# Half of a weight pair's combinations formed by an accumulating DMA, and another order of the seven products

## The chip, the cores and the metric

The kernel runs on one core of a Trainium2 chip. The metric is the device time of one execution in microseconds, as the median of several runs. TensorE (PE), VectorE (DVE), ScalarE (ACT), GpSimd (POOL) and the DMA queue of SyncE (SP) each work through their own list of instructions in order, and wait for each other by semaphores.

## What is computed

The reference runs two blocks on a sequence of 512 tokens of width 1024. The first has two layers modulated by a condition vector (one with differential attention and a gated delta rule, one with neighbourhood attention); the second has 2 hybrid layers (forgetting attention beside retention). All four layers end in a gated feed-forward network (FFN), and it is there, and in the projections that feed the hybrid layers, that the changed code works:

```python
def hybrid_layer(h, attn_norm_g, w_in, b_fgate, ret_gn_g, w_out,
                 ffn_norm_g, w_gate, w_up, w_down, cos, sin):
    xn = rmsnorm(h, attn_norm_g)
    proj = jnp.einsum('bld,dc->blc', xn, w_in)
    ...
    hn = rmsnorm(h, ffn_norm_g)
    ff = jax.nn.silu(jnp.einsum('bld,df->blf', hn, w_gate)) * jnp.einsum('bld,df->blf', hn, w_up)
    return h + jnp.einsum('blf,fd->bld', ff, w_down)
```

## The kernel before

Every large product is taken in full precision out of three passes: a weight tile and an activation are each split into a high part (ScalarE casts, into `whi`) and a low part (VectorE subtracts, into `wlo` for weights), and TensorE multiplies high by high, high by low and low by high.

**A pair by seven products.** For the gate and the up projection of an FFN, one 128-column tile of `w_gate` and one of `w_up` form a pair, `ra` and `rb`, each 128 x 1024 (eight blocks of the contraction over 128). The tokens are cut in two halves, the contraction in two halves (columns 0 to 511 and 512 to 1023 of a tile: a0, a1 of `ra`, b0, b1 of `rb`). Instead of eight half-size products the function `seven` does seven, out of sums of weight quarters and sums of activation quarters (the latter made once per layer by `make_quads` and `end_quads`, lines to L861). One such product is 4 x 3 = 12 matmuls with 128x256 outputs (L890), a pair 84. The weight sums are formed on GpSimd, in f32: L872 writes the high half of `s23` (a0 - b0), L873 adds b1 onto b0 in place (the sum is called rb' here), L874 writes the low half of `s23` (rb' - a0), L875 writes `s4` (a1 minus that low half). Then come, in program order, the split of `ra` and the products p1, p2; the split of `s23` and p6, p7; the split of `rb` and p5, p4; the split of `s4` and p3. ScalarE casts at L880, VectorE makes the low part at L881. Between the products the results are added: `u` is a copy of p1 (L901), L905 adds p6 to it, L909 makes v of p5 and u, L910 adds p7 to u, and `put` (L931) adds a last product and stores one quarter of the result; SiLU is at L933, gate times up at L936, the split of the hidden tile at L938 and L939.

**Where pairs stand.** Each of the four FFNs has 22 pairs of tiles. The first three go by another, slower way while the quarter sums of the activations are made; the other 19 go through `fast_pair`, which loads the two tiles (L924, L925) and calls `seven`. They stand in groups (one pair left of the first four; then 4, 4, 4 and 6). After every pair `work` runs down projections of the group before (`fm_group`, load L446, cast L462, low part L463, matmul L592, 24 matmuls each): two per pair in groups of four, one per pair for the last four pairs of the last group. `hy_two` does 10 pairs in each of the two hybrid layers, with its own loads (L1657).

**Buffers.** Raw weight tiles rotate through four buffers `wraw`, high and low parts through three each (`top.whi_65` to `67`, `top.wlo_68` to `70`). `s23` and `s4` take rings `ws` (1024 wide) and `w4` (512 wide), two buffers each in an FFN and one each in the hybrid layers. At the start of an FFN these rings lie in memory that the making of the activations' quarter sums still holds; L861 (`end_quads`) and L727 (the slow way's hidden tile) are VectorE's last instructions on it.

**Order.** A scheduler reorders the instructions of each engine by priorities, with the program order as a base; what an engine does next is then fixed. In the middle of an FFN TensorE's order per pair is p1 p2 p6 p7 p5 p4 p3 and two down projections. `ra` lies in the third high buffer, `s23` in the first, `rb` in the second; `s4` takes the third when p1 has read its half.

Of the kernel before, what the change touches and what calls it, by code (L numbers as in the profile page):

```python
# [16 lines left out]
ALU = mybir.AluOpType  # L17
# [6 lines left out]
T = 512  # L24
# [202 lines left out]
class K:  # L227
# [635 lines left out]
            T[1][1].append(dl)  # L863
        self.free(first)

    def seven(self, ra, rb, hi, lo, quads, h, put):


        nc = self.nc
        T = quads[0]  # L870
        s23, s4 = self.ring("ws"), self.ring("w4")
        nc.gpsimd.tensor_sub(s23[:, 512:], ra[:, :512], rb[:, :512])  # L872
        nc.gpsimd.tensor_add(rb[:, :512], rb[:, :512], rb[:, 512:])  # L873
        nc.gpsimd.tensor_sub(s23[:, :512], rb[:, :512], ra[:, :512])  # L874
        nc.gpsimd.tensor_sub(s4, ra[:, 512:], s23[:, :512])  # L875

        def split(src):
            m = src.shape[-1]
            wh, wl = self.weight("whi"), self.weight("wlo")
            nc.scalar.copy(wh[:, :m], src)  # L880
            nc.vector.tensor_sub(wl[:, :m], src, wh[:, :m].bitcast(F32))  # L881
            return wh, wl

        def product(w, o, x):
            ps = self.ps("L")[:, :h]
            for k in range(4):
                wc = slice(o + k * P, o + (k + 1) * P)
                for ww, xx, st, sp in ((w[0], x[0], k == 0, False), (w[0], x[1], False, False),
                                       (w[1], x[0], False, k == 3)):
                    nc.tensor.matmul(ps, ww[:, wc], xx[k], start=st, stop=sp)  # L890
            return ps

        def part(k0, c0):
            return [[x[k][:, c0:c0 + h] for k in range(k0, k0 + 4)] for x in (hi, lo)]

        t = self.ring("sp")
        u, v = t[:, :h], t[:, h:2 * h]
        w = split(ra)
        p1 = product(w, 0, part(0, 0))
        p2 = product(w, 512, part(4, 0))  # L900
        nc.scalar.copy(u, p1)  # L901
        put(0, 0, p2, u)
        w = split(s23)
        p6 = product(w, 0, T[2])
        nc.vector.tensor_add(u, p6, u)  # L905
        p7 = product(w, 512, T[3])
        w = split(rb)
        p5 = product(w, 0, T[1])
        nc.vector.tensor_add(v, p5, u)  # L909
        nc.vector.tensor_add(u, p7, u)  # L910
        put(1, 1, p7, v)
        p4 = product(w, 512, T[4])
        put(1, 0, p4, u)
        w = split(s4)
        p3 = product(w, 0, part(4, h))
        put(0, 1, p3, v)

    def fast_pair(self, gate, up, hi, lo, quads, h, hh, hl):

        nc = self.nc  # L920
        self.stream("L", "ffn")
        n = 2 * h
        rg, ru = self.weight("wraw"), self.weight("wraw")
        nc.sync.dma_start(rg, gate)  # L924
        nc.sync.dma_start(ru, up)  # L925
        sg, su = self.ring("sg"), self.ring("su")

        def put(tile, half, ps, more):
            c = slice(half * h, half * h + h)
            dst = (su if tile else sg)[:, c]  # L930
            nc.vector.tensor_add(dst, ps, more)  # L931
            if not tile:
                nc.scalar.activation(dst, dst, AF.Silu)  # L933

        self.seven(rg, ru, hi, lo, quads, h, put)
        nc.vector.tensor_mul(sg[:, :n], sg[:, :n], su[:, :n])  # L936
        th, tl = self.rslot("hh"), self.rslot("hl")
        nc.scalar.copy(th[:, :n], sg[:, :n])  # L938
        nc.vector.tensor_sub(tl[:, :n], sg[:, :n], th[:, :n].bitcast(F32))  # L939
        hh.append(th)  # L940
        hl.append(tl)
# [702 lines left out]
    def hy_two(self, l, js, hi, lo, outs, acts=(AF.Copy, AF.Copy)):  # L1644

        nc = self.nc
        quads = self.hyq
        if quads is None:
            for j, o, act in zip(js, outs, acts):
                def evict(i, ps, c0):  # L1650
                    nc.scalar.activation(o[:, c0:c0 + ps.shape[1]], ps, act)
                self.hy_tile(l, j, hi, lo, evict)
            return
        h = TB // 2
        ra, rb = self.weight("wraw"), self.weight("wraw")
        for t, j in zip((ra, rb), js):
            nc.sync.dma_start(t, self.a["w_hy"][l, j])  # L1657

        def put(tile, half, ps, more):
            dst = outs[tile][:, half * h:half * h + h]  # L1660
            nc.vector.tensor_add(dst, ps, more)
            if acts[tile] != AF.Copy:
                nc.scalar.activation(dst, dst, acts[tile])

        self.seven(ra, rb, hi, lo, quads, h, put)

    def v_tokens(self, f, stream):

# [168 lines left out]
    def ret_head(self, l, h, q, k, v, gate):  # L1837
# [45 lines left out]
        for i in range(5):  # L1883
# [18 lines left out]
                 w4=(512, 2)), LIN[1])  # L1902
# [495 lines left out]
```

## Time and profile before

| | us |
|---|---|
| median of 3 runs | 3403.38 |
| runs, lowest and highest | 3396.11, 3406.44 |
| profiled execution | 3402.65 |
| its span in the trace | 3400.7 |
| TensorE busy in the span | 3261.2 |
| VectorE, ScalarE, GpSimd busy | 2373.1, 1478.8, 879.7 |

The span is what the trace covers; the profiled execution's own time is 1.95 us longer. Four stretches of the span are the FFNs from their first fast pair on: 720 to 1000, 1680 to 1970, 2380 to 2640 and 3060 to 3350 us. What lies between is attention, recurrences, norms and projections. Idle time of an engine other than TensorE is of interest only where TensorE waits for it. GpSimd's idle time in the table of waits is for the most part a wait for a pair's tiles to land.

### The profile page before, as it was taken

The page shows a single profiled execution, that of the slowest core. Times are in us where ns is not written, and L with a number is a line of the kernel's source. Part 1 is how long each engine was busy: PE and PEld are TensorE (multiplying, and loading weights), DVE is VectorE, ACT ScalarE, POOL GpSimd, SP SyncE. Part 2 cuts the span into 40 slices and gives each one's busy share as a digit, 9 for nine tenths or more (in the row PEclk, how much of TensorE's full clock was granted, in tenths as well). Part 3 has the DMA queues.
Part 4 walks back from the last instruction along what each step waited for, and adds up shares of the span by engine and source line. Part 5 has one row for each costly group of instructions (what it writes and reads, how often), then busy time and mean ns, then how long its engine had stood idle before and what let it go on. Part 6 is the DMA issues. An engine that isn't in the chain of part 4 may idle for free.

```text
span 3400.7 us, 64156 instructions
## 1 busy us (share of the span) xinstructions
PE 3261.2 (96%) x25466; PEld 3021.2 (89%) x25466; DVE 2373.1 (70%) x4863; ACT 1478.8 (43%) x2767; POOL 879.7 (26%) x772
## 2 busy tenths in 40 slices
PE   7999999989999999999899999999999999999998
PEld 6877777789999789998899998879999988799998
DVE  7566757677786565445777876877777667788775
ACT  4455442354444344434544444434444444344444
POOL 0000252023342011110233432423333224313332
PEclk9999989999999999999999999999999999999999
DMA  5111254523334874111233342223333412132332
GB/s 219 43 37 61 87 174 152 167 91 100 103 109 145 308 235 129 60 49 43 90 104 102 99 150 66 66 73 97 100 103 100 158 51 69 57 119 88 103 106 92
DMA packets 144348, 365.95 MB, mean 108 GB/s; under 512 B 30368, under 2 KB 33440, under 8 KB 144048
## 3 DMA queue, kind: packets, MB, share of 16 engines
q1 hardware_dynamic: 136704, 352.63, 32.1%
q10 hardware_dynamic: 7344, 9.23, 0.9%
q8 instruction: 200, 3.28, 0.4%
q14 instruction: 100, 0.82, 0.1%
HBM read 342.75 MB, written 19.04 MB: 106 GB/s over the span
## 4 chain that ended last, share of the span: by engine, by line
PE 73%; DVE 9%; issue 4%; ACT 3%; DMA 3%; POOL 1%; DVEq 0%; ACTq 0%; POOLq 0%; SPq 0%
PE ffn.L L592 22%; PE ffn.L L890 21%; PE outp.L L592 4%; PE naproj.L L656 3%; PE retproj.L L890 3%; PE gproj.L L592 3%; PE foxproj.L L890 2%; PE foxproj.L L592 2%; PE fox.A L1794 1%; DVE top.wlo L881 1%; PE ret.B L1871 1%; PE fox.Ao L1820 1%; PE naattn.Ao L1626 1%; PE retproj.L L592 1%; DMA top.wraw<-in_w_hy_dram 1%
## 5 line engine op out<-in xcount | busy, mean ns | idle before, releaser
L463 DVE TENSOR_TENSOR top.wlo<-top.wraw,top.whi 128x512 fp32r<-128x512 f32 (+2 forms) x365 | 353.3, 970 | 181.8 <-ACT top.whi L462 171.7
L462 ACT CAST top.whi<-top.wraw 128x512 fp32r<-128x512 f32 (+2 forms) x365 | 282.1, 774 | 392.2 <-PE ffn.L L890 139.7
L890 PE MATMUL ffn.L<-outp.zone,top.whi 128*128 128x256 f32 (+1 forms) x2052 | 436.0, 283 | 10.4 <-ACT top.whi L880 10.4
L592 PE MATMUL ffn.L<-ffn.zone,top.whi 128*128 128x256 f32 (+1 forms) x2102 | 435.3, 282 | 0.0
L890 PEld LDWEIGHTS ffn.L<-outp.zone,top.whi 128*128 128x128 f32 x2052 | 338.5, 190 | 11.2 <-ACT top.whi L880 11.2
L592 PEld LDWEIGHTS ffn.L<-ffn.zone,top.whi 128*128 128x128 f32 x2102 | 341.9, 189 | 0.6 <-ACT ffn.zone L551 0.4
L880 ACT CAST top.whi<-top.wraw 128x1024 fp32r<-128x1024 f32 x192 | 201.5, 1050 | 322.1 <-PE ffn.L L890 137.0
L890 PE MATMUL ffn.L<-outp.zone,top.wlo 128*128 128x256 f32 (+1 forms) x1140 | 322.5, 283 | 1.5 <-DVE top.wlo L881 1.5
L592 PE MATMUL ffn.L<-ffn.zone,top.wlo 128*128 128x256 f32 (+1 forms) x1132 | 319.4, 282 | 0.3 <-DVE top.wlo L463 0.3
L881 DVE TENSOR_TENSOR top.wlo<-top.wraw,top.whi 128x1024 fp32r<-128x1024 f32 x192 | 270.6, 1409 | 68.2 <-ACT top.whi L880 66.5
L890 PE MATMUL ffn.L<-norm.zone,top.whi 128*128 128x256 f32 (+1 forms) x1406 | 285.7, 283 | 2.4 <-ACT top.whi L880 2.4
L872 POOL TENSOR_TENSOR top.zone<-top.wraw,top.wraw 128x512 f32<-128x512 f32 x78 | 108.1, 1386 | 612.9 <-DMA top.wraw<-in_w_up_dram 415.3
L592 PE MATMUL ffn.L<-outp.zone,top.whi 128*128 128x256 f32 (+1 forms) x1058 | 253.1, 283 | 0.2 <-ACT top.whi L462 0.2
L890 PEld LDWEIGHTS ffn.L<-norm.zone,top.whi 128*128 128x128 f32 x1406 | 226.3, 189 | 2.6 <-ACT top.whi L880 2.6
L890 PEld LDWEIGHTS ffn.L<-outp.zone,top.wlo 128*128 128x128 f32 x1140 | 216.1, 190 | 1.9 <-DVE top.wlo L881 1.9
L592 PEld LDWEIGHTS ffn.L<-ffn.zone,top.wlo 128*128 128x128 f32 x1132 | 213.3, 188 | 0.8 <-DVE top.wlo L463 0.8
L592 PEld LDWEIGHTS ffn.L<-outp.zone,top.whi 128*128 128x128 f32 x1058 | 183.0, 189 | 6.8 <-issue 5.6
L890 PE MATMUL ffn.L<-norm.zone,top.wlo 128*128 128x256 f32 (+1 forms) x608 | 171.8, 283 | 0.8 <-DVE top.wlo L881 0.8
L873 POOL TENSOR_TENSOR top.wraw<-top.wraw 128x512 f32<-128x512 f32 x96 | 135.8, 1415 | 7.5
L656 PE MATMUL naproj.L<-top.whi,outp.zone 128*128 128x256 f32 x544 | 134.9, 285 | 0.0
L874 POOL TENSOR_TENSOR top.zone<-top.wraw,top.wraw 128x512 f32<-128x512 f32 x78 | 123.1, 1578 | 32.9 <-DVE ada.zone L861 17.1
L592 PE MATMUL gproj.L<-dproj.zone,top.whi 128*128 128x256 f32 (+1 forms) x512 | 129.8, 342 | 0.0
(1791 smaller groups left out, 9493.5 us busy)
## 6 DMA issues: line engine op xcount, KB each, us to landing
top.wraw<-in_w_up_dram SPq DMA_DIRECT2D x220, 512.0 KB, 3.5
top.wraw<-in_w_dn_dram SPq DMA_DIRECT2D x160, 256.0 KB, 2.7
top.zone<-in_ada_w_dram SPq DMA_DIRECT2D x64, 512.0 KB, 5.2
top.wraw<-in_w_hy_dram SPq DMA_DIRECT2D x58, 512.0 KB, 3.5
top.wraw<-in_w_dn_dram SPq DMA_DIRECT2D x49, 384.0 KB, 3.1
top.wraw<-in_ada_w_dram SPq DMA_DIRECT2D x32, 512.0 KB, 4.6
top.wraw<-in_w_ho_dram SPq DMA_DIRECT2D x36, 256.0 KB, 2.8
top.wraw<-in_w_gdn_dram SPq DMA_DIRECT2D x17, 512.0 KB, 3.5
```

The costliest lines, as they stand in the source:

```text
L462: nc.scalar.copy(hi[:, :m], raw[:, c:c + m])
L463: nc.vector.tensor_sub(lo[:, :m], raw[:, c:c + m], hi[:, :m].bitcast(F32))
L592: nc.tensor.matmul(ps[:, :n], w[:, wc], x[ks[j]][:, c0:c0 + n], start=a, stop=b)
L656: nc.tensor.matmul(pst[t][:, :256], cols(x, k, t), ww[:, wc], start=a, stop=b)
L872: nc.gpsimd.tensor_sub(s23[:, 512:], ra[:, :512], rb[:, :512])
L873: nc.gpsimd.tensor_add(rb[:, :512], rb[:, :512], rb[:, 512:])
L874: nc.gpsimd.tensor_sub(s23[:, :512], rb[:, :512], ra[:, :512])
L880: nc.scalar.copy(wh[:, :m], src)
L881: nc.vector.tensor_sub(wl[:, :m], src, wh[:, :m].bitcast(F32))
L890: nc.tensor.matmul(ps, ww[:, wc], xx[k], start=st, stop=sp)
L1626: nc.tensor.matmul(po[:, j * P:(j + 1) * P], vv[kt // 3][:, kt % 3, hh * P:(hh + 1) * P], dt[:, i * P:(i + 1) * P], start=i == 0, stop=i == 3)
L1794: nc.tensor.matmul(ss[r][:, off[i] + a:off[i] + b], fq[fs, i * P:n], fk[fs, a:b], start=True, stop=b < n)
```

## The change

`seven` gets the DRAM addresses of the two tiles and loads them itself (L872, L873, SP's queue as before). Then GpSimd issues a DMA that reads b1 (columns 512 to 1023 of the second tile, 256 KB) from DRAM a second time and adds it onto columns 0 to 511 of the loaded tile (L875): rb' = b0 + b1 comes from there, and no longer from an addition on GpSimd. Three operations are left on GpSimd, with other names and widths: `s2` = a0 - rb' (L877, 512 wide, ring `w4`), and in one 1024 wide buffer of ring `ws` the halves `s34` = [b1 + s2 | a1 + s2] (L878, L879). Since s2 is the negative of the former low half of `s23`, p6 is now subtracted (L909). b1 + s2 is the former high half of `s23`, for p7; a1 + s2 is the former `s4`, for p3. The product order in the program is p1 p2 (`ra`), p6 (`s2`), p5 (`rb`), p7 (`s34`), p4 (`rb`), p3 (`s34`). Casts are at L884 and low parts at L885; L912 makes v of p5, L915 adds p7; `put` is at L932.

```diff
--- before.py
+++ after.py
@@ -863,16 +863,20 @@
-    def seven(self, ra, rb, hi, lo, quads, h, put):
+    def seven(self, a, b, hi, lo, quads, h, put):
 
 
         nc = self.nc
         T = quads[0]
-        s23, s4 = self.ring("ws"), self.ring("w4")
-        nc.gpsimd.tensor_sub(s23[:, 512:], ra[:, :512], rb[:, :512])
-        nc.gpsimd.tensor_add(rb[:, :512], rb[:, :512], rb[:, 512:])
-        nc.gpsimd.tensor_sub(s23[:, :512], rb[:, :512], ra[:, :512])
-        nc.gpsimd.tensor_sub(s4, ra[:, 512:], s23[:, :512])
+        ra, rb = self.weight("wraw"), self.weight("wraw")
+        nc.sync.dma_start(ra, a)
+        nc.sync.dma_start(rb, b)
+
+        nc.gpsimd.dma_start(rb[:, :512], b[:, 512:], accum_op=ALU.add)
+        s2, s34 = self.ring("w4"), self.ring("ws")
+        nc.gpsimd.tensor_sub(s2, ra[:, :512], rb[:, :512])
+        nc.gpsimd.tensor_add(s34[:, :512], rb[:, 512:], s2)
+        nc.gpsimd.tensor_add(s34[:, 512:], ra[:, 512:], s2)
 
         def split(src):
             m = src.shape[-1]
@@ -900,19 +904,19 @@
         p2 = product(w, 512, part(4, 0))
         nc.scalar.copy(u, p1)
         put(0, 0, p2, u)
-        w = split(s23)
+        w = split(s2)
         p6 = product(w, 0, T[2])
-        nc.vector.tensor_add(u, p6, u)
-        p7 = product(w, 512, T[3])
+        nc.vector.tensor_sub(u, u, p6)
         w = split(rb)
         p5 = product(w, 0, T[1])
         nc.vector.tensor_add(v, p5, u)
+        w2 = split(s34)
+        p7 = product(w2, 0, T[3])
         nc.vector.tensor_add(u, p7, u)
         put(1, 1, p7, v)
         p4 = product(w, 512, T[4])
         put(1, 0, p4, u)
-        w = split(s4)
-        p3 = product(w, 0, part(4, h))
+        p3 = product(w2, 512, part(4, h))
         put(0, 1, p3, v)
```

`fast_pair` and `hy_two` lose their two loads and pass the addresses on. The rest of the program is the same.

On GpSimd, where the second FFN's first two pairs stand (the first pair has the tiles `wraw_63` and `64` and the buffer `top.zone_73`, the second `wraw_61`, `62` and `top.zone_74`; the `naproj.zone` are the two `w4` buffers), before:

```order
L872 TENSOR_TENSOR top.zone_74<-top.wraw_61,top.wraw_62 128x512
L873 TENSOR_TENSOR top.wraw_62<-top.wraw_62 128x512
L874 TENSOR_TENSOR top.zone_74<-top.wraw_62,top.wraw_61 128x512
L875 TENSOR_TENSOR naproj.zone_13191<-top.wraw_61,top.zone_74 128x512
L872 TENSOR_TENSOR top.zone_73<-top.wraw_63,top.wraw_64 128x512
L873 TENSOR_TENSOR top.wraw_64<-top.wraw_64 128x512
L874 TENSOR_TENSOR top.zone_73<-top.wraw_64,top.wraw_63 128x512
L875 TENSOR_TENSOR naproj.zone_13191<-top.wraw_63,top.zone_73 128x512
```

and now:

```order
L875 DMA top.wraw_62<-in_w_up_dram 128x512
L877 TENSOR_TENSOR naproj.zone_13191<-top.wraw_63,top.wraw_64 128x512
L877 TENSOR_TENSOR naproj.zone_13191<-top.wraw_61,top.wraw_62 128x512
L878 TENSOR_TENSOR top.zone_73<-top.wraw_64,naproj.zone_13191 128x512
L879 TENSOR_TENSOR top.zone_74<-top.wraw_61,naproj.zone_13191 128x512
L878 TENSOR_TENSOR top.zone_74<-top.wraw_62,naproj.zone_13191 128x512
L879 TENSOR_TENSOR top.zone_73<-top.wraw_63,naproj.zone_13191 128x512
```

The two pairs' four operations each stood one pair after the other; now both short tiles come first, and the halves of the two long tiles are interleaved, the first pair's last. The DMAs of both pairs stand ahead of them.

On VectorE in the first FFN's middle, from the low part of the second tile on (`quads.zone_6832` are the `w4` buffers and parts of u and v, `top.zone_74` a `ws` buffer or one of the results), before:

```order
L881 TENSOR_TENSOR top.wlo_69<-top.wraw_64,top.whi_66 128x1024
L881 TENSOR_TENSOR top.wlo_70<-quads.zone_6832,top.whi_67 128x512
L931 TENSOR_TENSOR top.zone_74<-ffn.L_7358,quads.zone_6832 128x256
L905 TENSOR_TENSOR quads.zone_6832<-ffn.L_7376,quads.zone_6832 128x256
L463 TENSOR_TENSOR top.wlo_68<-top.wraw_61,top.whi_65 128x512
L909 TENSOR_TENSOR quads.zone_6832<-ffn.L_7405,quads.zone_6832 128x256
L910 TENSOR_TENSOR quads.zone_6832<-ffn.L_7390,quads.zone_6832 128x256
L931 TENSOR_TENSOR top.zone_75<-ffn.L_7390,quads.zone_6832 128x256
L463 TENSOR_TENSOR top.wlo_69<-top.wraw_62,top.whi_66 128x512
```

and now:

```order
L885 TENSOR_TENSOR top.wlo_69<-top.wraw_64,top.whi_66 128x1024
L932 TENSOR_TENSOR top.zone_74<-ffn.L_7358,quads.zone_6832 128x256
L885 TENSOR_TENSOR top.wlo_70<-top.zone_74,top.whi_67 128x1024
L909 TENSOR_TENSOR quads.zone_6832<-quads.zone_6832,ffn.L_7376 128x256
L463 TENSOR_TENSOR top.wlo_68<-top.wraw_61,top.whi_65 128x512
L912 TENSOR_TENSOR quads.zone_6832<-ffn.L_7392,quads.zone_6832 128x256
L463 TENSOR_TENSOR top.wlo_69<-top.wraw_62,top.whi_66 128x512
L915 TENSOR_TENSOR quads.zone_6832<-ffn.L_7408,quads.zone_6832 128x256
L932 TENSOR_TENSOR top.zone_75<-ffn.L_7408,quads.zone_6832 128x256
```

The second split of the group, L881 of `s4` 512 wide, is now L885 of `s34`, 1024 wide, and stands behind the add of the first output quarter instead of ahead of it. The subtraction of p6 follows that split.

## Rows read from the trace of the kernel before

**Rows 1.** The page: busy time (share of the span) and instructions; chain by engine.

```profile
PE 3261.2 (96%) x25466; PEld 3021.2 (89%) x25466; DVE 2373.1 (70%) x4863; ACT 1478.8 (43%) x2767; POOL 879.7 (26%) x772
...
PE 73%; DVE 9%; issue 4%; ACT 3%; DMA 3%; POOL 1%; DVEq 0%; ACTq 0%; POOLq 0%; SPq 0%
```

**Rows 2.** Stretches: length, busy us (instructions) of PE, PEld, DVE, ACT, POOL; clock, DMA, GB/s.

```profile
2380.00:2640.00 260.00, 260.00 (x2139) 260.00 (x2138) 196.66 (x310) 108.58 (x166) 94.61 (x68) 1.00 0.33 100
2640.00:3060.00 420.00, 398.90 (x2938) 359.49 (x2937) 309.48 (x741) 182.32 (x378) 119.78 (x110) 0.97 0.29 91
```

**Rows 3.** Timeline, POOL, first FFN's middle: start us, us, operation, [idle before <-releaser].

```profile
808.86 1.29 POOL L872 TENSOR_TENSOR top.zone<-top.wraw,top.wraw 128x512 f32<-128x512 f32 x1 [9.90 <-DMA top.wraw<-in_w_up_dram]
810.22 1.30 POOL L873 TENSOR_TENSOR top.wraw<-top.wraw 128x512 f32<-128x512 f32 x1
811.60 1.62 POOL L874 TENSOR_TENSOR top.zone<-top.wraw,top.wraw 128x512 f32<-128x512 f32 x1
813.29 1.29 POOL L875 TENSOR_TENSOR quads.zone<-top.wraw,top.zone 128x512 f32<-128x512 f32 x1
```

**Rows 4.** Timeline, SP's queue, there: a pair's first tile.

```profile
815.73 0.33 SPq L924 DMA_DIRECT2D top.wraw<-in_w_up_dram  x1
```

**Rows 5.** Timeline, ACT, there: casts of s23, the second tile, s4, the next first tile.

```profile
815.81 1.05 ACT L880 CAST top.whi<-top.zone 128x1024 fp32r<-128x1024 f32 x1 [1.53 <-PE ffn.L L592]
...
818.62 1.05 ACT L880 CAST top.whi<-top.wraw 128x1024 fp32r<-128x1024 f32 x1 [1.23 <-PE ffn.L L592]
820.10 0.62 ACT L880 CAST top.whi<-quads.zone 128x512 fp32r<-128x512 f32 x1 [0.43 <-PE ffn.L L890]
...
828.53 1.05 ACT L880 CAST top.whi<-top.wraw 128x1024 fp32r<-128x1024 f32 x1 [2.21 <-PE ffn.L L890]
```

**Rows 6.** Timeline, DVE, there: low parts of the first and the second tile.

```profile
814.00 1.67 DVE L881 TENSOR_TENSOR top.wlo<-top.wraw,top.whi 128x1024 fp32r<-128x1024 f32 x1 [0.58 <-ACT top.whi L880]
...
819.70 1.23 DVE L881 TENSOR_TENSOR top.wlo<-top.wraw,top.whi 128x1024 fp32r<-128x1024 f32 x1
```

**Rows 7.** Timeline, PE, there: end of the second product; fifth product.

```profile
821.25 0.28 PE L890 MATMUL ffn.L<-outp.zone,top.wlo 128*128 128x256 f32 x1
...
824.40 0.28 PE L890 MATMUL ffn.L<-outp.zone,top.wlo 128*128 128x256 f32 x1
```

**Rows 8.** Timeline, PE: after its pauses at FFN starts and the last FFN's end.

```profile
762.22 1.65 PE L890 MATMUL ffn.L<-outp.zone,top.whi 128*128 128x256 f32 x6 [3.73 <-ACT top.whi L880]
...
1687.33 1.44 PE L890 MATMUL ffn.L<-outp.zone,top.whi 128*128 128x256 f32 x5 [5.56 <-ACT top.whi L880]
...
3338.90 0.50 PE L890 MATMUL ffn.L<-norm.zone,top.whi 128*128 128x256 f32 x2 [2.44 <-ACT top.whi L880]
```

**Rows 9.** Timeline, POOL: first and second FFN's start.

```profile
755.26 1.34 POOL L875 TENSOR_TENSOR quads.zone<-top.wraw,top.zone 128x512 f32<-128x512 f32 x1 [14.40 <-DVE outp.zone L861]
...
1677.54 1.35 POOL L874 TENSOR_TENSOR top.zone<-top.wraw,top.wraw 128x512 f32<-128x512 f32 x1 [17.11 <-DVE ada.zone L861]
```

**Rows 10.** Timeline, ACT: last FFN's end.

```profile
3337.29 0.62 ACT L462 CAST ffn.zone<-top.wraw 128x512 fp32r<-128x512 f32 x1 [6.48 <-DMA top.wraw<-in_w_dn_dram]
```

**Rows 11.** DMA issues: destination<-source, queue, operation, count, KB each, median us to landing.

```profile
top.wraw<-in_w_up_dram SPq DMA_DIRECT2D x220, 512.0 KB, 3.5
top.wraw<-in_w_dn_dram SPq DMA_DIRECT2D x160, 256.0 KB, 2.7
...
top.wraw<-in_w_dv_dram SPq DMA_DIRECT2D x4, 512.0 KB, 7.5
```

**Rows 12.** Timeline, last FFN's last pairs: POOL, SP's queue, ACT.

```profile
3312.73 1.62 POOL L872 TENSOR_TENSOR ret.zone<-top.wraw,top.wraw 128x512 f32<-128x512 f32 x1 [7.25 <-DMA top.wraw<-in_w_up_dram]
...
3325.91 1.35 POOL L872 TENSOR_TENSOR top.zone<-top.wraw,top.wraw 128x512 f32<-128x512 f32 x1 [6.79 <-DMA top.wraw<-in_w_up_dram]
...
3322.31 0.33 SPq L925 DMA_DIRECT2D top.wraw<-in_w_up_dram  x1
...
3325.13 0.62 ACT L880 CAST top.whi<-norm.zone 128x512 fp32r<-128x512 f32 x1
```

More of the change, by code (lines that the diff above doesn't have):

```diff
@@ L922, in fast_pair @@
         n = 2 * h
-        rg, ru = self.weight("wraw"), self.weight("wraw")
-        nc.sync.dma_start(rg, gate)
-        nc.sync.dma_start(ru, up)
         sg, su = self.ring("sg"), self.ring("su")
@@ L933, in put @@
                 nc.scalar.activation(dst, dst, AF.Silu)
-        self.seven(rg, ru, hi, lo, quads, h, put)
+        self.seven(gate, up, hi, lo, quads, h, put)
         nc.vector.tensor_mul(sg[:, :n], sg[:, :n], su[:, :n])
@@ L1654, in hy_two @@
         h = TB // 2
-        ra, rb = self.weight("wraw"), self.weight("wraw")
-        for t, j in zip((ra, rb), js):
-            nc.sync.dma_start(t, self.a["w_hy"][l, j])
         def put(tile, half, ps, more):
@@ L1663, in put @@
                 nc.scalar.activation(dst, dst, acts[tile])
-        self.seven(ra, rb, hi, lo, quads, h, put)
+        self.seven(*(self.a["w_hy"][l, j] for j in js), hi, lo, quads, h, put)
     def v_tokens(self, f, stream):
```

## Prediction

> **What bounds the kernel now.** The page's first table says that TensorE is busy for 96% of the span, and the chain of work that ended last runs over it for 73% [rows 1]. So only two kinds of time can change: gaps of TensorE, and work put into its stream. The change adds no matmul and takes none away (84 per pair of weight tiles in both), so I looked for gaps stage by stage in the stretches table. In the third FFN TensorE is busy for 260.00 of 260.00 us; in a hybrid layer's attention and projections for 398.90 of 420.00 [rows 2]. In the middle of an FFN there is thus nothing to win, only slack to lose; something can be won where a feed-forward starts or ends, and in the hybrid stages.
>
> **What it removes.** Four GpSimd operations per pair, in the FFN's middle 1.29 + 1.30 + 1.62 + 1.29 = 5.5 us [rows 3], for 96 pairs; three stay, with their gaps about 4.3 us. TensorE does not wait for them there: the last ends at 814.58, and its result is cast at 820.10 [rows 3, 5], when TensorE lets go of the weight buffer. Price of what is removed: nothing in the middle, since the 5.5 us of slack hide it.
>
> **What it adds: X.** A DMA of 256 KB that adds onto the landed tile, issued by GpSimd, which stands between the landing of a pair's second tile and GpSimd's first operation. Let X be its time from that landing to its own. No row of before has an accumulating DMA or one that GpSimd issues. Bounds: a plain load of the same size lands in 2.7 us, one of twice the size in 3.5, and the slowest group of weight loads in 7.5 [rows 11]. An accumulation reads as well as writes its destination, so I take X = 5, between the second and the third (an estimate), and keep 2.7 and 7.5 for the range.
>
> **What X does in the middle of an FFN.** The second tile has landed at 808.86, where GpSimd begins now [rows 3]. The sum is there at 808.86 + X, s34 some 4.3 later: 813.16 + X. The earliest moment at which s34 can be cast is the end of the second product, whose last matmul starts at 821.25 and runs 0.28, so 821.53 [rows 7]. That leaves X up to 8.4. s2 is ready at 808.86 + X + 1.36 = 815.2 for a cast at 815.81 [rows 5]; it may slip by some 4 us, since s2 is wanted only after the two products of ra. The first tile's buffer is read by GpSimd to the end: its next load, issued at 815.73 today [rows 4], is issued at about 818.2 and lands 3.5 later [rows 11], at 821.7, for the cast that stands at 828.53 [rows 5], with 6.8 us of room. With X = 5: nothing, in some 60 of the 76 FFN pairs.
>
> **What X does in a feed-forward's last four pairs.** Only one w_dn projection follows each of them; the last of the fourth FFN takes 13.18 us (3312.73 to 3325.91) and the next pair's second tile goes into the buffer of this pair's first, which is issued at 3322.31 today and lands at 3325.91 [rows 12]. Now it must also wait for GpSimd's last read of that buffer, at 3312.73 + X + 4.3 = 3322.0 for X = 5: no delay. The loop becomes X + 4.3 + 3.7 = X + 8.0, which drifts from X = 5.2 on; s34's cast, at 3325.13 + 1.4 = 3326.5 [rows 12], leaves a further 4.5 us in the first pair. At X = 5: nothing. At X = 7.5 the drift is 2.3 a pair against 2.0 of room, so over four pairs about 5 us per FFN, 20 in all.
>
> **The other order of products.** p6, p5, p7, p4, p3 replace p6, p7, p5, p4, p3. The short tile, split last, was s4, 512 wide; now it is s34, 1024 wide, and it is wanted by the fifth product. From 821.53: cast 1.05 (as the cast at 818.62), 0.05, low part 1.23 (as at 819.70) [rows 5, 6] ends at 823.86. The fifth product's first matmul with a low part starts at 824.40 [rows 7], and its weights are loaded one matmul (0.12) earlier: 0.4 us of room. Cost: nothing, with a cover of 0.4 us. DVE puts the add of the first output ahead of this split and p6's subtraction behind it (the order rows of the change), and neither is on the path. If the split takes 1.67, as one that meets a GpSimd operation does [rows 3, 6] (the one at 814.00, beside GpSimd from 813.29 to 814.58), the room is gone; GpSimd is done by 818.2 at X = 5, so it does not meet it.
>
> The Trainium skill ("SBUF — State Buffer", "Who interferes with whom") says that a DVE instruction with two SBUF inputs contends with a GpSimd instruction that reads SBUF; the 1.67 against 1.23 us agree. By the same section a DMA that stalls under DVE work was one whose descriptors GpSimd writes, though it exempts DVE's two-input operations, an inference of its own; no row here shows one. By the first rule alone the sum is unchanged, by the second X would be at its upper end.
>
> **Where a feed-forward starts.** There is an idle stretch of 3.73 us in the first and 5.56 in the second [rows 8]; both end with the cast of s23, which waits for GpSimd, which waits until the buffers of the seven-product operands are free: 755.26 in the first, 1677.54 in the second [rows 9]. Afterwards the short tile s2 comes first and lets p6 and p5 run (2.82 us); p7 waits for s34. In the order rows s34 is finished as the sixth operation from that point, since the next pair's stand between. Second FFN: 1677.54 + 6 × 1.35 = 1685.6, cast to 1686.7, low part to 1687.9; TensorE is done with p2 at 1687.33 − 5.56 = 1681.8 and with p5 at 1684.6, so it idles 2.1 and then about 1.0 for the low part: 3.1 against 5.56, **gain 2.4** (0.8 if s2's buffer comes free with the next of DVE's operations, some 1.6 us later). First FFN: 755.26 + 8.1 = 763.4, to 764.4 and 765.6, against p5's end at 758.5 + 2.8 = 761.3: 3.1 + 1.0 = 4.1 against 3.73, **loss 0.4**. In the third the first accumulating DMA stands on GpSimd ahead of a small operation of the norm; I take **0.5** lost (0 to 1).
>
> **The last feed-forward's end.** TensorE idles 2.44 us there for the cast of the last pair's first tile [rows 8], which stands on ScalarE behind a cast that waits 6.48 us for its own load [rows 10]. The scheduler now puts the pair's cast first. **Gain 2.5** (0 to 3).
>
> **Hybrid layers**, 20 pairs: single buffers for s2 and s34, and GpSimd's other operations queue behind the wait for the sum. How the 21 idle us of the stretch in [rows 2] (and about as many in the other layer) change is open; I take 0, and ±5.
>
> **Sum.** +0.4 − 2.4 + 0.5 − 2.5 = −4.0, against the profiled execution's 3402.65 (0.7 under the median of the runs): 3398.7. Predicted **3399**.
>
> **Rivals.** *The accumulate lands late.* The point is X about 6.3, where four pairs' drift eats the room at a feed-forward's end; at 7.5 it costs 20 us (3419), and above 8.4 each further us costs a us in some 60 pairs more (X = 10: 1.6 × 60 = 96, and 4.8 us of drift in each of 16 pairs: about 3570). For it: no row shows X, and GpSimd is the issuer. Against: the queues' rows up to 3.5 us. Chance 0.17. *s34's split is late for p7.* The point is 0.4 us beyond 823.86; at 0.2 us too much in each of 76 pairs 15 us, 3414. For it: splits of 1.67 and more exist. Against: GpSimd is quiet at that moment unless X is above 8. Chance 0.10. *More is won than counted:* DVE, with fewer GpSimd operations beside it, lets TensorE's operands come earlier in the hybrid stages, and a fifth to two fifths of their 42 idle us go: 8 to 16 us, 3383 to 3391. Against: TensorE waits for other things there. Chance 0.23. *The sum is not off GpSimd's path:* if issuing costs GpSimd the 1.2 us saved, nothing changes in the middle, since slack hides both: within the forecast.
>
> **Chances.** The forecast with ±6 holds 0.50. A measurement here tells some 0.3% (10 us) from no change. Faster by more: 0.23; within: 0.49; slower by more: 0.28, the two slow rivals with the hybrid stages' bad side. The range reaches from 3384 (most of the gain rival) to 3423 (X up to 7.5, and s34 late).
>
> **What would show it.** Right: the pairs' period in the FFN's middle stays at 15.6 us, TensorE idles about 3 us at the second FFN's start and below 1 at the last one's end, and DMAs from GpSimd land in about 5 us. Wrong: p7's matmuls idle for the low part of s34 in every pair; the period of a feed-forward's last pairs above 13.2; GpSimd's first operation waiting for the accumulating DMA beyond 8 us.

## The result, and the profile after

The changed kernel takes 3427.75 us (median of four runs, 3426.37 to 3428.73) against 3402.99 for the kernel before on the same chip (four runs, one more than in the table ahead of the prediction): ratio 1.0074 [1.0058, 1.009], **slower by 25 us**, and outside the predicted range. The profiled execution has a span of 3425.8 us, 25.1 more than before.

The page of the changed kernel, in three pieces: busy time of the engines; the DMA queue that GpSimd issues to (packets, MB, share); DMA issues (count, KB each, median us from issue to landing):

```profile
PE 3271.0 (95%) x25466; PEld 3028.1 (88%) x25466; DVE 2387.0 (70%) x4863; ACT 1484.0 (43%) x2771; POOL 838.6 (24%) x772
...
q0 software_dynamic: 13824, 25.17, 4.6%
...
top.wraw<-in_w_dn_dram SPq DMA_DIRECT2D x160, 256.0 KB, 3.3
top.wraw<-in_w_up_dram POOLq DMA_DIRECT2D x76, 256.0 KB, 4.7
```

The number of matmuls is the one in [rows 1], and GpSimd is relieved by 41 us, which was of no use. The new DMA lands in 4.7 us in the median, near the 5 that the prediction took for X.

**Where the 25 us lie.** TensorE runs the same 25,466 matmuls in every kernel here, so the same-numbered matmul can be compared: the table gives how much later (+) than before a kernel gets through each stage, in us of the profiled executions, and below it the measured ratio. Executions of one kernel spread by up to 23 us, so entries of 1 to 3 us say little; what repeats from kernel to kernel counts. The profiled executions of e2, e4 and e10 lie 7, 11 and 12 us below their kernels' medians, so the ratio, not the sum of a column, tells what a kernel gains. e1 to e10 are the experiments.

| stage (before's time) | after | e1 | e9 | e2 | e4 | e3 | e5 | e6 | e7 | e8 | e10 |
|---|---|---|---|---|---|---|---|---|---|---|---|
| to the first FFN's pairs (0 to 750) | +4.0 | +5.2 | +5.3 | −0.8 | −1.8 | +4.6 | +2.8 | +3.4 | −1.8 | −0.1 | +1.7 |
| first FFN's start (750 to 780) | −1.2 | −0.8 | −0.9 | −1.1 | +0.4 | +0.4 | +0.3 | +0.1 | −1.2 | −1.2 | 0.0 |
| second FFN's start (1673 to 1705) | −7.1 | −7.1 | −7.0 | −7.0 | −7.0 | −0.5 | −7.1 | −7.1 | −7.0 | −7.1 | −7.1 |
| four FFN middles | +2.2 | +4.3 | +2.4 | −0.8 | −0.9 | +32.0 | −1.0 | +2.6 | −1.0 | +2.7 | +1.3 |
| **four FFN ends** (last four pairs) | **+22.0** | +13.6 | −4.7 | −2.2 | +1.2 | +11.8 | −4.4 | −2.1 | −4.3 | +43.6 | −3.3 |
| two hybrid stages | +6.3 | +6.1 | +4.8 | +10.8 | −0.8 | +0.8 | −4.9 | −3.0 | −4.7 | +3.3 | −5.4 |
| measured ratio | 1.0074 | 1.0056 | 0.9991 | 0.9994 | 0.9986 | 1.0157 | 0.9958 | 0.9976 | 0.9946 | 1.0127 | 0.9967 |

Of the change's 25 us, 22 lie in the four ends. In the kernel before, the first FFN's pairs run to 1038 us and the third's to 2658; the stretches given ahead of the prediction (720 to 1000, 2380 to 2640) stop short of them. The timeline of the changed kernel's first FFN end, engine by engine (start us, duration us, engine, line, operation, out<-in, [idle before <-releaser]):

```profile
1000.18 0.88 POOL L875 DMA_DIRECT2D top.wraw<-in_w_up_dram  x1 [3.85 <-DMA top.wraw<-in_w_up_dram]
1004.79 1.28 POOL L877 TENSOR_TENSOR quads.zone<-top.wraw,top.wraw 128x512 f32<-128x512 f32 x1 [3.74 <-DMA top.wraw<-in_w_up_dram]
...
1014.34 0.88 POOL L875 DMA_DIRECT2D top.wraw<-in_w_up_dram  x1 [5.22 <-DMA top.wraw<-in_w_up_dram]
```

```profile
1006.11 0.62 ACT L884 CAST top.whi<-quads.zone 128x512 fp32r<-128x512 f32 x1 [6.01 <-POOL quads.zone L877]
1006.63 1.04 ACT L884 CAST top.whi<-top.wraw 128x1024 fp32r<-128x1024 f32 x1
...
```

```profile
1006.76 1.23 DVE L885 TENSOR_TENSOR top.wlo<-quads.zone,top.whi 128x512 fp32r<-128x512 f32 x1 [4.21 <-ACT top.whi L884]
...
1008.25 1.95 DVE L885 TENSOR_TENSOR top.wlo<-top.wraw,top.whi 128x1024 fp32r<-128x1024 f32 x1
```

```profile
1010.26 0.33 SPq L873 DMA_DIRECT2D top.wraw<-in_w_up_dram  x1
```

```profile
1010.25 0.39 PE L894 MATMUL ffn.L<-outp.zone,top.wlo 128*128 128x256 f32 x1 [2.02 <-DVE top.wlo L885]
```

Read it along one turn. The second tile `rb` has landed at 1000.18, where GpSimd issues the adding DMA; the sum is there at 1004.79, X = 4.61. ScalarE does nothing for 6.01 us: the next cast in its list is that of `s2` (512 wide, from `quads.zone`), which needs the sum. The cast of `ra`, whose tile landed long ago, stands **behind** it and starts at 1006.63. `ra`'s low part ends at 1010.20, TensorE has waited 2.02 us for it, and the next `rb` load is issued at 1010.26, since its buffer is `ra`'s and the split was its last reader. That tile lands at 1014.34. A turn is thus 4.61 (X) + 1.32 (s2) + 0.52 (cast of s2) + 1.62 (cast of ra; VectorE's low part of s2 and an add) + 2.01 (low part, issue) + 4.08 (landing) = 14.16 us, and the next one 15.4, where TensorE's matmuls of a pair and one projection, 108 at 0.1175, take 12.7.

The price is not the pauses alone. Stretches of 10 us, after and then before (columns as in [rows 2]; behind the counts the granted clock):

```profile
1010.00:1020.00 10.00, 9.75 (x69) 9.75 (x70) 7.61 (x14) 4.23 (x7) 0.88 (x1) 0.83 0.54 133
```

```profile
1010.00:1020.00 10.00, 10.00 (x87) 10.00 (x87) 9.01 (x13) 4.88 (x7) 4.51 (x4) 1.00 0.58 181
```

Behind the pause of 2.02 us the clock granted in this stretch is 0.83 rather than 1.00: a part of it ran at the lower level, and 69 matmuls ran instead of 87. The second FFN's end shows this effect at its largest, in the changed kernel and then in e1, where the first tile's split comes first:

```profile
1923.00:1980.00 57.00, 52.73 (x418) 51.85 (x417) 42.52 (x64) 23.65 (x40) 17.86 (x14) 0.94 0.39 109
```

```profile
1921.00:1975.00 54.00, 50.80 (x413) 49.21 (x412) 44.62 (x64) 23.03 (x38) 19.96 (x14) 1.00 0.42 115
```

Over the four ends the clock is 0.97, 0.94, 0.97 and 1.00 in the changed kernel, 1.00 in all four of e1, and 1.00 in three and 0.97 in one before. An estimate from these shares and the lengths is 6.8 us lost to the lower level, against 1.6 before, so some 5 of the 22 us are the clock's. In the fourth end a pause of the same 2.02 us left the clock at 1.00.

### The profile page after: what moved, and what is told of

Its sections match the earlier page's. It is cut to its first block, busy times and chain, and to the rows that moved or that the text cites. A ratio compares the mean times of both kernels' runs of the same rounds, so it can differ in the third digit from the quotient of the medians.

```text
span 3425.8 us, 64253 instructions
## 1 busy us (share of the span) xinstructions
PE 3271.0 (95%) x25466; PEld 3028.1 (88%) x25466; DVE 2387.0 (70%) x4863; ACT 1484.0 (43%) x2771; POOL 838.6 (24%) x772
## 3 DMA queue, kind: packets, MB, share of 16 engines
q0 software_dynamic: 13824, 25.17, 4.6%
## 5 line engine op out<-in xcount | busy, mean ns | idle before, releaser
L463 DVE TENSOR_TENSOR top.wlo<-top.wraw,top.whi 128x512 fp32r<-128x512 f32 (+2 forms) x365 | 324.5, 891 | 163.2 <-ACT top.whi L462 156.9
L884 ACT CAST top.whi<-top.wraw 128x1024 fp32r<-128x1024 f32 x192 | 201.4, 1049 | 319.8 <-PE ffn.L L894 218.9
L894 PE MATMUL ffn.L<-outp.zone,top.wlo 128*128 128x256 f32 (+1 forms) x1140 | 325.6, 286 | 12.7 <-DVE top.wlo L885 12.5
L885 DVE TENSOR_TENSOR top.wlo<-top.wraw,top.whi 128x1024 fp32r<-128x1024 f32 x192 | 256.6, 1336 | 42.2 <-ACT top.whi L884 42.1
L875 POOL DMA_DIRECT2D top.wraw<-in_w_up_dram x76 | 67.4, 887 | 482.2 <-DMA top.wraw<-in_w_up_dram 449.8
L877 POOL TENSOR_TENSOR norm.zone<-top.wraw,top.wraw 128x512 f32<-128x512 f32 x58 | 85.3, 1471 | 244.8 <-DVE top.wlo L885 79.5
L884 ACT CAST top.whi<-top.zone 128x1024 fp32r<-128x1024 f32 x78 | 81.9, 1050 | 100.1 <-PE ffn.L L894 50.4
```

What stands on the lines that cost most here:

```text
L463: nc.vector.tensor_sub(lo[:, :m], raw[:, c:c + m], hi[:, :m].bitcast(F32))
L875: nc.gpsimd.dma_start(rb[:, :512], b[:, 512:], accum_op=ALU.add)
L877: nc.gpsimd.tensor_sub(s2, ra[:, :512], rb[:, :512])
```

## The experiments

**e1: the first tile's split first.** s2's split is queued behind that of `ra`; all else is as in the changed kernel.

```diff
-            nc.scalar.copy(wh[:, :m], src)
-            nc.vector.tensor_sub(wl[:, :m], src, wh[:, :m].bitcast(F32))
+            c = nc.scalar.copy(wh[:, :m], src)
+            d = nc.vector.tensor_sub(wl[:, :m], src, wh[:, :m].bitcast(F32))
+            self.last_split = c, d
...
+        first = self.last_split
...
-        w = split(s2)
+        w = None
+        with self.tc.issue_after(first[0].ins), self.tc.issue_after(first[1].ins):
+            w = split(s2)
```

> The changed kernel, with one constraint on issue order: s2's cast and low part are queued behind those of the pair's first tile. In the changed kernel the scheduler puts s2's cast ahead of the first tile's in the last three pairs of each FFN. Theory 'place': there ScalarE waits for the accumulating DMA with the first tile's cast queued behind it, and the next second tile's load waits for that first tile's split, so the DMA (about 5 us) is in a loop of some 15 us against 12.7 of matmuls. Then this gives back most of the losses at the FFNs' ends: 3405 to 3413 us. Theory 'landing': the loop over the reused buffer (load 4, sum 5, three GpSimd operations 4.4 = 13.4 us) is too long wherever s2 stands: 3422 or more. Theory 'products': the loss comes from the other product order (s34 split late, low parts stretched beside GpSimd): 3422 or more.

3420.95 us, ratio 1.0056 [1.0036, 1.0075]. The ends cost 13.6 us instead of 22.0, so the order of the casts is some 8 us of them, much of it the clock that it gives back, and something else holds the rest. The time lies between the ranges of the three theories (3405 to 3413, and 3422 or more). GpSimd and SP's queue in e1, one turn in the first FFN's end:

```profile
1002.58 0.89 POOL L875 DMA_DIRECT2D top.wraw<-in_w_up_dram  x1 [3.75 <-DMA top.wraw<-in_w_up_dram]
1006.75 2.36 POOL L877 TENSOR_TENSOR quads.zone<-top.wraw,top.wraw 128x512 f32<-128x512 f32 x1 [3.29 <-DMA top.wraw<-in_w_up_dram]
...
1010.44 1.75 POOL L879 TENSOR_TENSOR top.zone<-top.wraw,quads.zone 128x512 f32<-128x512 f32 x1
1017.18 0.88 POOL L875 DMA_DIRECT2D top.wraw<-in_w_up_dram  x1 [5.00 <-DVE top.wlo L885]
```

```profile
1012.21 0.33 SPq L873 DMA_DIRECT2D top.wraw<-in_w_up_dram  x1
```

Now the loop that the prediction priced stands alone. The next `rb` load is issued (1012.21) when GpSimd's last operation, which reads `ra`'s other half, ends (1012.19): 4.17 (X) + 5.44 (three operations) + 0.02 + 4.97 (from the load's issue to the next adding DMA) = 14.60 us. The last row names VectorE, but the load itself landed only 4.4 us after its issue, at 1016.65, so it is what closes the turn. This is the longest of e1's twelve turns in the four ends; they take 12.6 to 14.6 us, 13.8 in the mean. The prediction had 5 + 4.3 + 3.7 = 13.0.

**e2 to e4: one part of the change at a time.** In e2 the half sum is an addition on GpSimd again, with the new operands and order; e3 has the accumulating DMA with the operands and order of before; e4 has a DMA from GpSimd of the same bytes that doesn't add, so it leaves out the half sum and computes other numbers.

```diff
# e2, on the changed kernel
-        nc.gpsimd.dma_start(rb[:, :512], b[:, 512:], accum_op=ALU.add)
+        nc.gpsimd.tensor_add(rb[:, :512], rb[:, :512], rb[:, 512:])
# e3, on the kernel before
+        nc.gpsimd.dma_start(rb[:, :512], b[:, 512:], accum_op=ALU.add)
-        nc.gpsimd.tensor_sub(s23[:, 512:], ra[:, :512], rb[:, :512])
-        nc.gpsimd.tensor_add(rb[:, :512], rb[:, :512], rb[:, 512:])
         nc.gpsimd.tensor_sub(s23[:, :512], rb[:, :512], ra[:, :512])
+        nc.gpsimd.tensor_sub(s23[:, 512:], rb[:, 512:], s23[:, :512])
# e4, on the changed kernel
-        nc.gpsimd.dma_start(rb[:, :512], b[:, 512:], accum_op=ALU.add)
+        nc.gpsimd.dma_start(rb[:, :512], b[:, 512:])
```

> The changed kernel, with the half sum made by an addition on GpSimd (1.3 us) in place of the accumulating DMA; product order, and s2's place ahead of the first tile in the last three pairs, as in the changed kernel. 'Place' and 'landing': without the DMA both loops fall below 12.7 us: 3398 to 3408. 'Products': 3420 or more.

3402.32 us, ratio 0.9994 [0.998, 1.0008], 25 us below the changed kernel. Without the DMA the ends are −2.2, though the product order is the new one: the DMA is what makes them long.

> The accumulating DMA and three GpSimd operations, but the former operands (s23, s4) and the former product order p6 p7 p5 p4 p3; the first tile's cast then stands ahead of s23's everywhere. 'Place': 3403 to 3413. 'Landing': 3420 or more. 'Products': 3403 or less.

3453.54 us, ratio 1.0157 [1.0125, 1.019]. That is above 3420, as the theory 'landing' had it, but the ends are the smaller part (11.8): with the old operands and order the middles pay as well, 9.8 to 11.5 us in three of the four, and nothing in the third FFN, whose period is 16.1. ScalarE, SP's queue and GpSimd of e3 in the first FFN's middle:

```profile
908.56 1.05 ACT L884 CAST top.whi<-top.zone 128x1024 fp32r<-128x1024 f32 x1 [6.18 <-POOL top.zone L878]
...
910.03 1.04 ACT L884 CAST top.whi<-top.wraw 128x1024 fp32r<-128x1024 f32 x1
```

```profile
913.42 0.33 SPq L873 DMA_DIRECT2D top.wraw<-in_w_up_dram  x1
```

```profile
901.20 0.89 POOL L875 DMA_DIRECT2D top.wraw<-in_w_up_dram  x1 [8.44 <-DMA top.wraw<-in_w_up_dram]
...
917.13 0.89 POOL L875 DMA_DIRECT2D top.wraw<-in_w_up_dram  x1 [7.35 <-DMA top.wraw<-in_w_up_dram]
```

The cast of the wide s23 waits 6.18 us for the DMA and two operations; `rb`'s cast stands behind it, and the next `rb` load behind `rb`'s split. The turn is 15.9 us, the next 16.6, where the matmuls' period is 15.6. The short s2, which needs one operation after the sum, is thus what lets the middle hide the DMA (32.0 us against 2.2 in the changed kernel).

> The changed kernel with the GpSimd-issued DMA as a plain copy onto the same half tile (nothing is added, so the half sum is left out and the numbers computed are others). If adding is what makes it long, it lands about 3 us after issue instead of 4.7, and the time falls by about 2 us for each of some 12 pairs' loop turns, to 3405 to 3415. If issue from GpSimd is what makes it long, it lands in 4 to 5 us and the time stays at 3420 to 3430.

3403.73 us, ratio 0.9986 [0.9969, 1.0004]: the loss is gone, with a little more than was expected. The page of e4:

```profile
q0 software_dynamic: 7680, 25.17, 2.3%
...
top.wraw<-in_w_up_dram POOLq DMA_DIRECT2D x76, 256.0 KB, 3.6
```

With 1.1 us less from issue to landing a turn in the first FFN's end is 12.6 to 13.4 us, and the ends cost 1.2. So not the second fetch and not its issue from GpSimd, but the microsecond that adding takes carries the turn past TensorE's 12.7.

**e9: the first tile's buffer freed one operation earlier.** On top of e1 the two halves of s34 change places, so that GpSimd's last operation reads `rb`.

```diff
-        nc.gpsimd.tensor_add(s34[:, :512], rb[:, 512:], s2)
         nc.gpsimd.tensor_add(s34[:, 512:], ra[:, 512:], s2)
+        nc.gpsimd.tensor_add(s34[:, :512], rb[:, 512:], s2)
```

> Run e1_ra_first with the two additions of s34 exchanged: the one that reads the pair's first tile runs before the one that reads the second, so the buffer into which the next pair's second tile is loaded is free some 1.3 to 1.7 us earlier. Theory 'buffer loop' (in an FFN's last four pairs: load, sum, GpSimd's reads, next load; 13.3 to 14.6 us a turn in e1): each turn 1.3 to 1.7 shorter, 13 us lost at the FFNs' ends become 2 to 6: 3408 to 3414. If it is not this buffer that holds the loads back: within 3 us of e1 (3418 to 3424).

3401.86 us, ratio 0.9991 [0.9975, 1.0008], 19 us below e1, with an accumulating DMA that is as slow as before; 3408 to 3414 had been expected. GpSimd and SP's queue:

```profile
1000.27 0.88 POOL L875 DMA_DIRECT2D top.wraw<-in_w_up_dram  x1 [2.17 <-DMA top.wraw<-in_w_up_dram]
...
1006.50 2.16 POOL L878 TENSOR_TENSOR top.zone<-top.wraw,quads.zone 128x512 f32<-128x512 f32 x1
1008.62 1.73 POOL L879 TENSOR_TENSOR top.zone<-top.wraw,quads.zone 128x512 f32<-128x512 f32 x1
1012.71 0.89 POOL L875 DMA_DIRECT2D top.wraw<-in_w_up_dram  x1 [2.35 <-DVE ffn.zone L944]
```

```profile
1008.69 0.33 SPq L873 DMA_DIRECT2D top.wraw<-in_w_up_dram  x1
```

The load leaves at 1008.69, when L878 is done, with L879 still to come. The turn is 12.4, others 12.1 and 11.9; the ends go to −4.7, where twelve turns shorter by 1.3 to 1.7 us give 16 to 20. With e1 this settles the two causes: both need the adding DMA (e2, e4), and each edit takes its own share away.

**e8: another slot for the next second tile.** On top of e1 one buffer of the ring is skipped in the last pairs, so that the next `rb` doesn't land in `ra`'s.

```diff
+        if done >= 19:
+            self.wnext["wraw"] += 1
```

> The changed kernel with the first tile's cast first (run e1_ra_first) and, in the last three pairs of each FFN, one raw weight buffer skipped per pair, so that a pair's second tile is loaded into the former pair's second buffer, which is free earlier, and not into its first, which GpSimd reads last. Theory 'landing' (the reuse of that buffer closes a loop of load 4 to 5, sum 5, GpSimd 4.4 us): gives back most of the 13.6 us that e1 still loses at the four FFNs' ends: 3405 to 3413. If something else holds the last pairs back (transfers slowed by the accumulation): 3418 to 3424.

3448.78 us, ratio 1.0127 [1.0103, 1.0151]: no improvement, and outside both expectations. SP's queue and GpSimd of e8 (its lines are two further down):

```profile
1025.75 0.33 SPq L875 DMA_DIRECT2D top.wraw<-in_w_up_dram  x1
```

```profile
1013.58 0.88 POOL L877 DMA_DIRECT2D top.wraw<-in_w_up_dram  x1 [7.10 <-DMA top.wraw<-in_w_up_dram]
...
1029.54 0.89 POOL L877 DMA_DIRECT2D top.wraw<-in_w_up_dram  x1 [7.23 <-DMA top.wraw<-in_w_up_dram]
```

The next `rb` now lands in this pair's own `rb` buffer, which is freed only by `rb`'s split, near the end of the pair: a turn of 16 us, and 43.6 us in the ends. That makes another and longer loop of the same kind: the load waits for the last reader of the buffer it lands in.

**e5, e6, e7, e10: what is worth keeping.** e5 is e2 with the former function in the 20 hybrid pairs. e6 adds to e5 the accumulating DMA in the first 15 pairs of each FFN. e7 is e5 with e1's edit. e10 is e7 with the DMA in all FFN pairs and e9's exchange.

```diff
# e5, in the hybrid pairs
-        self.seven(*(self.a["w_hy"][l, j] for j in js), hi, lo, quads, h, put)
+        self.seven_old(ra, rb, hi, lo, quads, h, put)
# e6, on e5
-        nc.gpsimd.tensor_add(rb[:, :512], rb[:, :512], rb[:, 512:])
+        if self.late_pair:
+            nc.gpsimd.tensor_add(rb[:, :512], rb[:, :512], rb[:, 512:])
+        else:
+            nc.gpsimd.dma_start(rb[:, :512], b[:, 512:], accum_op=ALU.add)
```

> The kernel with the half sum by GpSimd (run e2_pool_sum) and, in the hybrid layers' 20 pairs, the former function with its operands and order. In e2's trace the two hybrid stages are 5.2 and 5.6 us longer than before, as in the changed kernel (5.5 in the first). If the new product order costs that there: 3402 - 11 = 3388 to 3395. If the hybrid stages vary by themselves from build to build: 3400 to 3405.

> As e5_hybrid_old, but with the accumulating DMA in each FFN's first 15 fast pairs, and GpSimd's addition in the last four and nowhere else. If the DMA costs nothing in the middle of an FFN, as the prediction says: within 4 us of e5_hybrid_old. If it also costs there (low parts stretched, transfers slowed): 8 us or more above e5.

> As e5_hybrid_old, with s2's cast and low part queued behind the first tile's. If s2's place costs at an FFN's end without the DMA too (e2 lost 3.5 us at the first FFN's end): 3 to 5 us below e5. If place matters only where s2 is late: within 2 us of e5.

> e7_pool_ra_first (former function in the hybrid layers, first tile's cast first) with the accumulating DMA in all fast pairs of the FFNs in place of GpSimd's addition, and the exchange of e9. With e9's gain: the DMA's middle (about 5 us, e6 against e5) and what is left at the ends over e7's 3387: 3392 to 3399. Without it: 3402 to 3408.

e5 3390.53 us, ratio 0.9958 [0.9941, 0.9974]; e6 3395.36, 0.9976 [0.9962, 0.999]; e7 **3386.8**, 0.9946 [0.9923, 0.9968]; e10 3395.22, 0.9967 [0.9954, 0.998]. In the middle the DMA costs 5 us by the medians (e6 against e5, between the two expectations; the intervals overlap), and the middles go from −1.0 to +2.6, so it seems not quite free there. In all FFN pairs, with the loop mended, it costs 8 by the medians of e10 and e7; the middles and ends of their traces hold 3 of them, and where the rest lies is not shown. That e7 is 3.7 below e5 does not show that s2's place costs without the DMA: their ends are alike (−4.3 and −4.4), and their profiled executions differ by 4.6 ahead of the first FFN. e7, which has no accumulating DMA and GpSimd's addition again, beats both kernels: 18 us below before. The hybrid stages prefer the former order by 12 us (e5 against e2, by the medians; 16 by the traces).

## Why the prediction was wrong

**The step that failed is "what X does in a feed-forward's last four pairs"**: nothing at X = 5, with a drift only from 5.2 on. It cost 22 us, and for two reasons.

*The order of the casts was not read there.* The sum let `ra`'s split run early, as before. But the scheduler gives the splits another order in the last three pairs of each FFN: ScalarE's list in the build of the changed kernel, in the middle and then in the first of those pairs (`wraw_3` is `ra` above and `wraw_2` below):

```
L884 CAST top.whi_7_67<-top.wraw_3_63 128x1024
L884 CAST top.whi_5_65<-quads.zone_706_6832 128x512
L884 CAST top.whi_6_66<-top.wraw_4_64 128x1024
...
L884 CAST top.whi_7_67<-quads.zone_706_6832 128x512
L884 CAST top.whi_6_66<-top.wraw_2_62 128x1024
L884 CAST top.whi_5_65<-top.wraw_3_63 128x1024
```

Before, `ra` came first there too. This could be read ahead of the prediction, which showed the order at an FFN's start and middle alone, and at the last FFN's end even counted the pair's cast coming first as a gain of 2.5. e1 prices it: 8.4 of the 22.0 us by the traces, 6 us by the two ratios.

*The loop was priced too short and held against too long a period.* It was X + 8.0, and was to drift from X = 5.2 on, that is against 13.18 us, the distance of two GpSimd rows in before's fourth FFN. But GpSimd waits for loads at both of them; TensorE's matmuls need 12.7 (13.1 in the third FFN), and the prediction's own 13.0 at X = 5 is above that. The term X was right: 5.05 in the mean of e1's twelve turns, 5.1 in the changed kernel's, 5 forecast. But the three operations took 4.8 in the mean instead of 4.3 (in the turn shown 5.44: L877 2.36, L879 1.75, both beside VectorE's operations), and from the load's issue to the next adding DMA it was 4.0 instead of 3.7. The loop is thus 13.8; twelve turns of 1.1 above 12.7 are 13 us, and e1's ends cost 13.6. The rival "the accumulate lands late" put its point at X = 6.3; with these terms the loop passes 12.7 from X = 3.9 on. The mechanism and the rival were right; the terms beside X and the period were not. The mark set for it, a period of the last pairs above 13.2, is what the trace shows (14.2 and 15.4). e9, which takes one operation out of the loop, returns all of it.

**What held.** X itself: 4.7 us in the median. The middle: the pairs' period is the one of before (15.6; 16.1 in the third FFN) but for a few pairs, in the first FFN three of 15.8, 16.0 and 16.7. These rows of the changed kernel's GpSimd show a usual turn:

```profile
813.39 0.87 POOL L875 DMA_DIRECT2D top.wraw<-in_w_up_dram  x1 [6.22 <-DMA top.wraw<-in_w_up_dram]
818.45 1.28 POOL L877 TENSOR_TENSOR quads.zone<-top.wraw,top.wraw 128x512 f32<-128x512 f32 x1 [4.18 <-DVE top.wlo L885]
...
828.99 0.87 POOL L875 DMA_DIRECT2D top.wraw<-in_w_up_dram  x1 [6.19 <-DMA top.wraw<-in_w_up_dram]
```

The Trainium skill ("SBUF — State Buffer", "Who interferes with whom") was weighed for X at its upper end by a stall of GpSimd's descriptors under VectorE's two-input work; at 4.7 us the trace shows no such stall, in line with the exemption that the section infers. The margin of 0.4 us of s34's split held on the whole: the four middles lose 2.2 us together, against 15 in that rival. That relief of GpSimd is worth nothing in the middle held too: e2, with four operations, has middles of −0.8. At the third FFN's start, where 0.5 was to be lost, nothing was.

**Terms of the sum that were mis-sized.** *The second FFN's start* gave 7.1 instead of 2.4. TensorE's rows there (after), and the stretch of before behind its pause of 5.56 us [rows 8]:

```profile
1699.74 0.39 PE L894 MATMUL ffn.L<-outp.zone,top.wlo 128*128 128x256 f32 x1 [0.71 <-DVE top.wlo L885]
```

```profile
1687.00:1692.00 5.00, 4.67 (x22) 4.67 (x23) 3.07 (x3) 1.21 (x3) 1.42 (x1) 0.50 0.36 108
```

The pause is 0.71 and not the 3.1 forecast, since four of the six operations counted between the wait and the finished s34 run ahead of the wait; two of them are these, the wait's own row is the third (GpSimd, after):

```profile
1685.10 1.47 POOL L878 TENSOR_TENSOR top.zone<-top.wraw,naproj.zone 128x512 f32<-128x512 f32 x1
1686.53 1.48 POOL L879 TENSOR_TENSOR top.zone<-top.wraw,naproj.zone 128x512 f32<-128x512 f32 x1
1691.66 1.56 POOL L878 TENSOR_TENSOR top.zone<-top.wraw,naproj.zone 128x512 f32<-128x512 f32 x1 [3.65 <-DVE ada.zone L861]
```

That is 4.85 us; the other 2.2 are the clock's, as far as an estimate tells. In before, 22 matmuls behind the long pause stand 0.21 apart instead of 0.12, some 2.1 us in all, at a granted clock of 0.50, which is the lower of its two levels; after the short pause it stays at 1.00. The prediction counted pauses and left the clock behind them out. Every kernel with the new order has the 7 us, e3 with the old one has not: it is the order's gain, and none of the DMA's.

*The first FFN's start* gave 1.2 instead of costing 0.4; the entries of the ten builds with the new order lie between −1.2 and +0.4, so little can be said of it. *The last FFN's end* was to give 2.5; there the changed kernel loses 2.2, while e2, e5 and e7 win 3.7 to 4.5. The gain existed, and the loop ate it.

*The hybrid stages*, 0 ± 5, cost 6.3 by the traces. In the first of them all kernels with the new order lose 3.7 to 6.1 us, by DMA or addition, the four with the former function win 2.0 to 3.7, and e3 (old order with the DMA) loses 0.6; in the second, new-order kernels lie between −4.5 and +5.6. So the order goes with the loss in the first; which wait it is, among many small ones, was not settled. Nor was it settled why the four with the former function, which run before's own code there, are faster than before.

*Code that the change doesn't touch*, up to the first FFN, is 4.0 us later in the changed kernel's execution; over the ten other builds this stretch lies between −1.8 and +5.3. It was no term of the sum, and no run tells its cause.

## What to carry to other kernels

Where a change puts a slower step between a landing and its first use, write down for the places with the least cover the whole loop (landing, step, last reader of the buffer, next load into it) with contended durations, and compare it with the period of the bounding engine; which operation reads a buffer last can be worth nearly as much as a faster step (e9: 19 us for two lines exchanged; e4: 24 for a DMA 1.1 us quicker). Read the order of every in-order engine at those places too: an operation that waits for the new step stops all that stands behind it, ready or not. Take the period from the bounding engine's own work, not from another engine's rows. And price a pause of TensorE together with the clock granted behind it.

## What the runs showed of the hardware

Adding on landing has a price: a DMA of 256 KB that GpSimd issues lands in 4.7 us with the addition and 3.6 without (FFN pairs, e4); GpSimd's issue row takes 0.88 us with it; and the queue counts 13,824 packets against 7,680 for the same 25.17 MB, with packet times of 4.6% of the 16 engines' span against 2.3%. The Trainium skill ("DMA: Bandwidth & Descriptors", "Anatomy of one DMA — SWDGE (gpsimd) path") gives 2.0 us and bytes over 436e3; an estimate by it for 256 KB is 2.6 us for any such DMA, under both measurements, and the measurements decide.

Operations of VectorE and of GpSimd that overlap are longer on both sides: `ra`'s low part takes 1.95 us instead of the 1.23 of [rows 6], GpSimd's L877 2.36 (e1) instead of 1.28 (the changed kernel), in the rows above. And the plain loads of the down projections, of the same 256 KB on SP's queue, land in 3.3 us instead of 2.7 [rows 11] in the changed kernel and e1 and 3.4 in e4, which fetch a quarter twice (3.0 to 3.4 in all the builds that do), and in 2.7 again in e2, e5 and e7, which don't.
